# Weight forms made by additions and adding transfers, with no plain units, in a retention and state-space block

## The chip, the cores and the metric

The kernel runs on one core of a Trainium2 chip. The metric is device time in microseconds (us) for one execution; the times shown are medians of several runs. A core has TensorE (matrix products into PSUM), VectorE, ScalarE and GpSimd (elementwise work), SyncE (which issues transfers), and sixteen DMA engines that move the data. In the profile these are PE (with PEld, its weight loads), DVE, ACT, POOL and SP.

## The reference

One layer of a hybrid encoder over 512 positions with 2048 channels, all float32:

```python
h = rmsnorm(x, norm1_w[l])
proj = jnp.einsum('bsd,de->bse', h, w_in[l])
q, k, v, g_ret, z, xbc, dt_raw, gate_r, gate_s = jnp.split(proj, offsets, axis=-1)
y_r = retention(q, k, v, positions) * silu(g_ret)
y_s = ssd(xbc, dt_raw, conv_w[l], conv_b[l], dt_bias[l], a_log[l], d_skip[l])
y_s = rmsnorm(y_s * silu(z), ssd_norm_w[l])
p_r = jnp.einsum('bse,ed->bsd', y_r, w_br_ret[l])
p_s = jnp.einsum('bse,ed->bsd', y_s, w_br_ssd[l])
merged = sigmoid(gate_r) * p_r + sigmoid(gate_s) * p_s
x = x + jnp.einsum('bsd,de->bse', merged, w_out[l])
return rmsnorm(x, norm_f_w)
```

The input projection has 22592 columns: q, k, v and a gate for 8 retention heads of 256; z (4096), xBC (4096 + 2 x 1024) and dt (64) for the state-space branch; two merge gates of 2048. The state-space branch has 64 heads of 64 channels in 8 groups. With a chunk's running sum `acum` of the step sizes times decay rates, its scan computes

```python
decay = jnp.exp(jnp.where(causal, seg, -jnp.inf))        # seg = acum[l] - acum[s]
y = jnp.einsum('blsg,blsgh,bsghp->blghp', cb, decay, xc)  # within a chunk
y = y + jnp.einsum('blgn,bghpn->blghp', cc, state) * jnp.exp(acum)[..., None]
state = state * exp(acum[:, -1]) + einsum('bsgn,bsgh,bsghp->bghpn', bc, tail, xc)
```

where xc is x times its step size and `tail` is the decay from a position to the end of its chunk. The kernel uses chunks of 128 positions here.

## The kernel before

**Products.** Nearly all the work is products of a weight block (2048 deep, 256 columns wide) with activations (2048 deep, 512 positions). One such product is a *unit* (function `unit`). Depth is taken in eight steps k of 256. In each step the weights and the activations are seen as 2 x 2 blocks, two halves of the depth by two halves of the columns or positions, and the product is made by the Strassen-Winograd scheme: seven block products of combined operands in place of eight. The table `SEVEN` lists them as (PSUM bank, half, weight form, activation form). Both operands carry seven forms in a tile's slots 0 to 6: four blocks, and combinations of them. Each form is split into a high part in a reduced format (`hi`, cast on ScalarE at L150) and the rest (`lo`, subtracted on VectorE at L151), and a product is three matmuls, hi x hi, hi x lo, lo x hi (L202 to L204). So a unit issues 8 x 7 x 3 matmuls of 256 columns. After the eight steps, `unit` combines the banks into the four output blocks (L255 to L259).

A *plain* unit makes all eight block products by the table `FOUR`, 8 x 4 x 3 matmuls of 512 columns, and needs no combined weight forms; its outputs are combined at L250 to L252. Which units are plain is set by hand: K and V of head 0 (`PLAIN_K`, `PLAIN_V`), the first of the two x units of each group (`PLAIN_X`), the last merge gate (`PLAIN_M`), and the first and last units of the later projections (`PLAIN2`). The last unit of all is written out by itself (`PASSES`) and is plain in the same sense.

**Weights.** Function `products` loads weights two steps at a time, a pair, into a tile `wf` with `FB` = 3 buffers: two loads of 256 KB on SP (L216), four of 128 KB where B and C share a unit. VectorE then forms slots 4 and 5 (L219), 0 (L221) and 6 (L222) for both steps, and then come the cast and the subtraction for each step, into tiles `whi` (`HB` = 7 buffers) and `wlo` (`LB` = 6). The weight work is issued at a raised priority, ahead of its use. In the last three steps (`LAST`) of a unit the products are ordered by bank, so that the first banks are finished early.

**Activations.** A stage's eight operand groups stay in tiles `hh0` to `hh7` and `hl0` to `hl7` while all of its units run. They have one buffer each, so the next stage's group i is written after the last unit of the stage before has used it. Forms 4 and 6 (`combined`, L155 and L156) are made on GpSimd for seven of the eight groups, forms 5 and 0 (`completed`, L159 and L160) on VectorE.

**Stages.** After the first norm come the 8 retention heads (four units each, with rotary tables, scores, values and a group norm), then 8 state-space groups, each with one unit for B and C, and twice a unit for x, one for z and, but for the first time, one for the merge gates (16 in all); then the projections of the retention output, of the two halves of the state-space output, and the output projection with the last norm.

**The scan.** For each 128 channels of x, a block with two heads, the convolved x is transposed and scaled (`xd`, L622), decayed on GpSimd (`xl`, L625), multiplied with B into the chunk states (L629, L636). For each of the two heads in turn, SP loads the running sums to all partitions (`L`, two buffers, L643), ScalarE makes four differences (L645) and one exponential (L647), VectorE multiplies by CB (L648), and TensorE makes the chunks' outputs (L650), 64 partitions for each head. State outputs (L654), skip, gate and a running sum of squares on GpSimd (L664) follow.

**Order.** Apart from a few sections whose order is written out (`InOrder`), a planner orders each engine's instructions by priority and simulated time when the kernel is built; on the chip each engine then runs its own list in that order.

Of the kernel before, what the change touches and what calls it, by code (L numbers as in the profile page):

```python
# [8 lines left out]
F32 = mybir.dt.float32  # L9
# [57 lines left out]
def constants():  # L67
# [7 lines left out]
    for h in range(NH):  # L75
# [17 lines left out]
SEVEN = (((0, 0, 1, 1), (1, 0, 3, 3), (1, 1, 0, 5)),  # L93
         ((2, 0, 5, 6), (2, 1, 4, 4)),
# [11 lines left out]
PLAIN2 = (0, 7)  # L106
PLAIN_Q, PLAIN_K, PLAIN_V, PLAIN_G = (), (0,), (0,), ()
PLAIN_B, PLAIN_X, PLAIN_Z, PLAIN_M = (), (0,), (), (15,)
# [21 lines left out]
def hybrid_block(tc, A, out):  # L130
# [43 lines left out]
    def rows(src, i):  # L174
        return src[i * 256:(i + 1) * 256, :].rearrange("(r p) t -> p r t", p=P)

# [12 lines left out]
    def products(H, parts, pt, groups, PE=PE, after=None):  # L189
# [17 lines left out]
        for k in range(NP):  # L207
            with tc.high_priority(offset=PRIO):
                if k % 2 == 0:
# [8 lines left out]
                    if not plain:  # L218
                        DVE.tensor_tensor(f2[:, :, 4:6, :], f2[:, :, 1:3, :],  # L219
                                          f2[:, :, 0:1, :].to_broadcast([P, 2, 2, P]), op=ALU.subtract)  # L220
                        DVE.tensor_tensor(f2[:, :, 0, :], f2[:, :, 2, :], f2[:, :, 4, :], op=ALU.add)  # L221
                        DVE.tensor_tensor(f2[:, :, 6, :], f2[:, :, 3, :], f2[:, :, 0, :], op=ALU.subtract)  # L222
# [16 lines left out]
    def unit(H, parts, alt=False, plain=False):  # L239
# [7 lines left out]
        with tc.high_priority():  # L247
            if plain:
                for c in range(2):
                    ACT.copy(o[:, 2 * c:2 * c + 2, :], pt[2 * c][:, 0:1, :].to_broadcast([P, 2, 256]))  # L250
                    DVE.tensor_tensor(o[:, 2 * c, :], pt[2 * c][:, 1, :], o[:, 2 * c, :], op=ALU.add)
                    DVE.tensor_tensor(o[:, 2 * c:2 * c + 2, :], pt[2 * c + 1], o[:, 2 * c:2 * c + 2, :], op=ALU.add)  # L252
            else:
                p1, u = o[:, 0, :], o[:, 0:4:3, :]
                ACT.copy(p1, pt[0][:, 0, :])  # L255
                DVE.tensor_tensor(o[:, 1:3, :], pt[1], p1[:, None, :].to_broadcast([P, 2, 256]), op=ALU.add)  # L256
                DVE.tensor_tensor(u, o[:, 2:3, :].to_broadcast([P, 2, 256]), pt[2], op=ALU.subtract)
                DVE.tensor_tensor(o[:, 2, :], o[:, 0, :], pt[2][:, 1, :], op=ALU.subtract)
                DVE.tensor_tensor(u, pt[3], u, op=ALU.add)  # L259
# [297 lines left out]
    with tc.tile_pool(name="ssd", bufs=1) as sp:  # L557
# [30 lines left out]
        for g in range(NG):  # L588
# [14 lines left out]
            for jj in range(2):  # L603
# [5 lines left out]
                for e in range(2):  # L609
# [15 lines left out]
                    POOL.tensor_tensor(xl, xd[:, :TB - 1], tail[:, :TB - 1, hs, None].to_broadcast([P, TB - 1, 2, 64]),  # L625
# [13 lines left out]
                    pi = att_tile()  # L639
                    for i in range(2):  # L640

                        L = sp.tile([P, TB, P], F32, name="L", bufs=2)
                        SP.dma_start(out=L.rearrange("p c l -> p (c l)"), in_=A_d[h0 + i].partition_broadcast(P))  # L643
                        for c in range(TB):
                            ACT.activation(L[:, c, :], L[:, c, :], AF.Relu, scale=-1.0,  # L645
                                           bias=At[:, c, h0 + i:h0 + i + 1])
                        ACT.activation(L, L, AF.Exp, scale=-1.0)  # L647
                        DVE.tensor_tensor(L, L, CB, op=ALU.mult)  # L648
                        for c in range(TB):
                            PE.matmul(pi[i * 64:(i + 1) * 64, c * P:(c + 1) * P], xd[:, c, i, :], L[:, c, :],  # L650
                                      start=True, stop=True)
# [65 lines left out]
    with tc.tile_pool(name="fin", bufs=1) as fp:  # L717
# [56 lines left out]
        dve.tensor_tensor(t0, o[0][:, 0:2, :], t0, op=ALU.add)  # L774
# [47 lines left out]
```

## Time and profile before

| | |
|---|---|
| median of 3 runs | 2779.19 us (2778.53 to 2781.94) |
| profiled execution | 2779.37 us, of which the span is 2777.6 us |
| mean granted TensorE clock | 0.991 |
| mean rate of all transfers | 131 GB/s |
| read from HBM, written to it | 321.56 MB, 37.49 MB |

The span runs from the first to the last instruction of the one execution that the profiler recorded. In rows of groups, a line names the source line, the engine, the operation, output<-inputs, the shape and the count; then come the busy time in us, the mean of one in ns, and the idle time of the engine just before them with what ended it. Rows of stretches give the busy time of each engine between two times. Rows of waits give the engine and line that waited, whom it waited for, the total in us, the count and the longest.

### The profile page before, as it was taken

Reading aid. Unit: us, or ns where it says so; the run is one execution under the profiler, and the core shown is the slowest. Engines: PE = TensorE matmul, PEld = TensorE weight load, DVE = VectorE, ACT = ScalarE, POOL = GpSimd, SP = SyncE. Lnnn points to the kernel's source line nnn. Section 1 sums busy time; section 2 is a strip of 40 time slices with the busy share of each in tenths; the row PEclk is TensorE's granted clock in tenths of the full one; section 3 lists DMA queues with packets and bytes.
Section 4 is the critical chain, followed back from the end, with each engine's and each line's share of the span. In section 5 each row is a group of like instructions: output and inputs, shape, how many; then the busy total and the mean of one; then the engine's idle time right before and its main releaser. Section 6 shows DMA issues by size and latency. Waiting matters only on the chain.

```text
span 2777.6 us, 52322 instructions
## 1 busy us (share of the span) xinstructions
PE 2715.8 (98%) x20508; PEld 2586.4 (93%) x20508; DVE 2391.4 (86%) x3782; ACT 1336.1 (48%) x1905; POOL 253.1 (9%) x206
## 2 busy tenths in 40 slices
PE   6999999999999999999999999999999999999898
PEld 3899999999989999999999999999989989889797
DVE  8999888888869798898979899797989798898997
ACT  4344333333355555555565555465554343533453
POOL 4000000000000000000000000000021020111321
PEclk9999999999999999999999999999999999999999
DMA  3333333333333434343434434344465554556634
GB/s 125 99 103 104 97 109 103 103 92 103 103 111 114 134 122 133 104 128 117 135 121 135 135 109 126 119 129 120 129 199 168 162 179 137 167 179 194 217 117 137
DMA packets 344375, 362.48 MB, mean 131 GB/s; under 512 B 25664, under 2 KB 298304, under 8 KB 344128
## 3 DMA queue, kind: packets, MB, share of 16 engines
q1 hardware_dynamic: 323888, 325.32, 38.7%
q10 hardware_dynamic: 20240, 33.82, 3.3%
q8 instruction: 161, 2.64, 0.4%
q14 instruction: 86, 0.70, 0.1%
HBM read 321.56 MB, written 37.49 MB: 129 GB/s over the span
## 4 chain that ended last, share of the span: by engine, by line
PE 82%; DVE 8%; DMA 5%; issue 3%; ACT 1%; POOL 1%; SPq 0%; DVEq 0%; POOLq 0%; ACTq 0%
PE pb L204 23%; PE pb L203 23%; PE pb L202 23%; PE att L202 2%; PE att L204 2%; PE att L203 2%; DVE wlo L151 2%; PE att L650 2%; DMA wf<-in_w_in_dram 1%; PE att L536 1%; PE att L521 1%; DMA wf<-in_w_br_ssd_dram 1%; DVE hl L151 1%; PE pb L120 1%; PE att L654 1%
## 5 line engine op out<-in xcount | busy, mean ns | idle before, releaser
L203 PE MATMUL pb<-hl,whi 128*128 128x256 f32 (+1 forms) x5464 | 1601.1, 294 | 11.9 <-DVE hl L120 9.3
L202 PE MATMUL pb<-hh,whi 128*128 128x256 f32 (+1 forms) x5464 | 1596.8, 295 | 9.9 <-ACT hh L150 7.1
L204 PE MATMUL pb<-hh,wlo 128*128 128x256 f32 (+1 forms) x5464 | 1587.9, 294 | 6.0 <-DVE wlo L151 6.0
L150 ACT CAST whi<-wf 128x896 fp32r<-128x896 f32 (+1 forms) x968 | 824.5, 888 | 870.1 <-PE pb L203 396.6
L203 PEld LDWEIGHTS pb<-hl,whi 128*128 128x128 f32 x5464 | 1049.1, 192 | 34.6 <-DVE hl L120 11.0
L202 PEld LDWEIGHTS pb<-hh,whi 128*128 128x128 f32 x5464 | 1046.4, 192 | 33.8 <-ACT hh L150 8.4
L151 DVE TENSOR_TENSOR wlo<-wf,whi 128x896 fp32r<-128x896 f32 (+1 forms) x968 | 1011.8, 1056 | 71.9 <-PE pb L204 30.6
L204 PEld LDWEIGHTS pb<-hh,wlo 128*128 128x128 f32 x5464 | 1041.0, 192 | 28.1 <-DVE wlo L151 6.8
L219 DVE TENSOR_TENSOR wf<-wf 128x512 f32<-128x512 f32 x404 | 281.5, 697 | 159.1 <-DMA wf<-in_w_in_dram 118.8
L202 PE MATMUL att<-hh,whi 128*128 128x256 f32 (+1 forms) x768 | 227.0, 297 | 1.4 <-ACT whi L150 1.4
L203 PE MATMUL att<-hl,whi 128*128 128x256 f32 (+1 forms) x768 | 226.7, 297 | 0.0
L204 PE MATMUL att<-hh,wlo 128*128 128x256 f32 (+1 forms) x768 | 222.7, 297 | 2.0 <-DVE wlo L151 2.0
L221 DVE TENSOR_TENSOR wf<-wf 128x256 f32<-128x256 f32 x404 | 174.3, 432 | 4.0
L222 DVE TENSOR_TENSOR wf<-wf 128x256 f32<-128x256 f32 x404 | 174.0, 431 | 3.1
L202 PEld LDWEIGHTS att<-hh,whi 128*128 128x128 f32 x768 | 147.4, 192 | 6.0 <-ACT whi L150 2.0
L204 PEld LDWEIGHTS att<-hh,wlo 128*128 128x128 f32 x768 | 144.8, 191 | 7.0 <-DVE wlo L151 2.8
L203 PEld LDWEIGHTS att<-hl,whi 128*128 128x128 f32 x768 | 147.5, 192 | 3.9
L645 ACT ACTIVATE L<-L,sst 128x128 f32<-128x128 f32 x256 | 80.3, 394 | 70.3 <-DMA L<-A_d 40.6
L625 POOL TENSOR_TENSOR xl<-xd,sst 128x384 f32<-128x384 f32 x32 | 33.7, 1054 | 864.1 <-DVE xd L622 864.1
L255 ACT COPY o<-pb 128x256 f32<-128x256 f32 x89 | 33.0, 370 | 128.0 <-PE pb L204 117.8
L256 DVE TENSOR_TENSOR o<-pb,o 128x512 f32<-128x512 f32 x89 | 61.0, 685 | 36.2 <-PE pb L204 35.9
L542 POOL TENSOR_TENSOR rs<-rs,mhalf 128x1 f32<-128x1 f32 x32 | 23.9, 751 | 713.3 <-DVE rs L541 704.2
(230 smaller groups left out, 2133.4 us busy)
## 6 DMA issues: line engine op xcount, KB each, us to landing
wf<-in_w_in_dram SPq DMA_DIRECT2D x640, 256.0 KB, 3.1
wf<-in_w_br_ssd_dram SPq DMA_DIRECT2D x128, 256.0 KB, 3.5
wf<-in_w_out_dram SPq DMA_DIRECT2D x72, 256.0 KB, 3.2
wf<-in_w_in_dram SPq DMA_DIRECT2D x128, 128.0 KB, 2.5
L<-A_d SPq DMA_DIRECT2D x64, 256.0 KB, 3.4
wf<-in_w_br_ret_dram SPq DMA_DIRECT2D x64, 256.0 KB, 3.5
ys_d<-B ACTq DMA_DIRECT2D x32, 256.0 KB, 2.5
E<-E_d SPq DMA_DIRECT2D x64, 96.0 KB, 2.7
```

Of the source, the lines that this page charges most:

```text
L150: ACT.copy(dst_hi, src)
L151: DVE.tensor_tensor(dst_lo, src, dst_hi.bitcast(F32), op=ALU.subtract)
L202: PE.matmul(o, wh, xh, start=b not in started, stop=False, skip_group_check=True)
L203: PE.matmul(o, wh, xl, start=False, stop=False, skip_group_check=True)
L204: PE.matmul(o, wl, xh, start=False, stop=(k == NP - 1), skip_group_check=True)
L219: DVE.tensor_tensor(f2[:, :, 4:6, :], f2[:, :, 1:3, :], f2[:, :, 0:1, :].to_broadcast([P, 2, 2, P]), op=ALU.subtract)
L221: DVE.tensor_tensor(f2[:, :, 0, :], f2[:, :, 2, :], f2[:, :, 4, :], op=ALU.add)
L222: DVE.tensor_tensor(f2[:, :, 6, :], f2[:, :, 3, :], f2[:, :, 0, :], op=ALU.subtract)
L256: DVE.tensor_tensor(o[:, 1:3, :], pt[1], p1[:, None, :].to_broadcast([P, 2, 256]), op=ALU.add)
L625: POOL.tensor_tensor(xl, xd[:, :TB - 1], tail[:, :TB - 1, hs, None].to_broadcast([P, TB - 1, 2, 64]), op=ALU.mult)
L645: ACT.activation(L[:, c, :], L[:, c, :], AF.Relu, scale=-1.0, bias=At[:, c, h0 + i:h0 + i + 1])
L650: PE.matmul(pi[i * 64:(i + 1) * 64, c * P:(c + 1) * P], xd[:, c, i, :], L[:, c, :], start=True, stop=True)
```

## The change

- No unit is plain any more: the `PLAIN` lists are empty, so all of `unit`'s products go by `SEVEN`.
- The signs of the scheme are changed, so that each combined weight form is a sum: forms 0 and 5 become sums of two blocks, 4 = new 0 + block 2, 6 = 4 + block 3. The activations' forms and the output additions take the other signs, with the same number of operations. Two entries of `SEVEN` change their weight slots.
- A third transfer on SP brings the first block of each step (512-byte rows) a second time, into slot 5 (`first_tiles`). Then POOL issues one transfer for each of the two steps that adds slots 1 and 2 to slots 0 and 5 on the way (`accum_op`), 128 KB each from SBUF to SBUF. VectorE makes two additions of 256 elements for the pair, where it made one of 512 and two of 256.
- The scan's `L` is one tile for both heads with one buffer, one transfer, one exponential and one product with CB; the matmuls with `xd` go chunk by chunk, the two heads in turn.
- `xl` is made on VectorE instead of GpSimd.

```diff
-SEVEN = (((0, 0, 1, 1), (1, 0, 3, 3), (1, 1, 0, 5)),
-         ((2, 0, 5, 6), (2, 1, 4, 4)),
+SEVEN = (((0, 0, 1, 1), (1, 0, 3, 3), (1, 1, 4, 5)),
+         ((2, 0, 5, 6), (2, 1, 0, 4)),
          ((3, 0, 6, 2), (3, 1, 2, 0)))
...
-PLAIN2 = (0, 7)
-PLAIN_Q, PLAIN_K, PLAIN_V, PLAIN_G = (), (0,), (0,), ()
-PLAIN_B, PLAIN_X, PLAIN_Z, PLAIN_M = (), (0,), (), (15,)
+PLAIN2 = ()
+PLAIN_Q, PLAIN_K, PLAIN_V, PLAIN_G = (), (), (), ()
+PLAIN_B, PLAIN_X, PLAIN_Z, PLAIN_M = (), (), (), ()
...
     def combined(f, eng):
-        eng.tensor_tensor(f[:, 4, :], f[:, 0, :], f[:, 2, :], op=ALU.add)
-        eng.tensor_tensor(f[:, 6, :], f[:, 0, :], f[:, 1, :], op=ALU.subtract)
+        eng.tensor_tensor(f[:, 4, :], f[:, 0, :], f[:, 2, :], op=ALU.subtract)
+        eng.tensor_tensor(f[:, 6, :], f[:, 0, :], f[:, 1, :], op=ALU.add)
 
     def completed(f, eng):
-        eng.tensor_tensor(f[:, 5, :], f[:, 4, :], f[:, 1, :], op=ALU.subtract)
-        eng.tensor_tensor(f[:, 0, :], f[:, 3, :], f[:, 5, :], op=ALU.subtract)
+        eng.tensor_tensor(f[:, 5, :], f[:, 2, :], f[:, 6, :], op=ALU.subtract)
+        eng.tensor_tensor(f[:, 0, :], f[:, 3, :], f[:, 5, :], op=ALU.add)
...
+    def first_tiles(src, i):
+        return src[i * 256:(i + 2) * 256, :P].rearrange("(m r p) t -> p m r t", r=2, p=P)[:, :, 0, :]
...
                     if not plain:
-                        DVE.tensor_tensor(f2[:, :, 4:6, :], f2[:, :, 1:3, :],
-                                          f2[:, :, 0:1, :].to_broadcast([P, 2, 2, P]), op=ALU.subtract)
-                        DVE.tensor_tensor(f2[:, :, 0, :], f2[:, :, 2, :], f2[:, :, 4, :], op=ALU.add)
-                        DVE.tensor_tensor(f2[:, :, 6, :], f2[:, :, 3, :], f2[:, :, 0, :], op=ALU.subtract)
+                        SP.dma_start(out=f2[:, :, 5, :], in_=first_tiles(parts[0], k))
+                        for m in range(2):
+                            POOL.dma_start(out=f2[:, m, 0:6:5, :], in_=f2[:, m, 1:3, :], accum_op=ALU.add)
+                        DVE.tensor_tensor(f2[:, :, 4, :], f2[:, :, 0, :], f2[:, :, 2, :], op=ALU.add)
+                        DVE.tensor_tensor(f2[:, :, 6, :], f2[:, :, 4, :], f2[:, :, 3, :], op=ALU.add)
...
-                    POOL.tensor_tensor(xl, xd[:, :TB - 1], tail[:, :TB - 1, hs, None].to_broadcast([P, TB - 1, 2, 64]),
+                    DVE.tensor_tensor(xl, xd[:, :TB - 1], tail[:, :TB - 1, hs, None].to_broadcast([P, TB - 1, 2, 64]),
                                        op=ALU.mult)
...
+                    L = sp.tile([P, 2, TB, P], F32, name="L")
+                    SP.dma_start(out=L.rearrange("p i c l -> p i (c l)"),
+                                 in_=A_d[hs, :].partition_broadcast(P))
                     for i in range(2):
-                        L = sp.tile([P, TB, P], F32, name="L", bufs=2)
-                        SP.dma_start(out=L.rearrange("p c l -> p (c l)"), in_=A_d[h0 + i].partition_broadcast(P))
                         for c in range(TB):
-                            ACT.activation(L[:, c, :], L[:, c, :], AF.Relu, scale=-1.0,
+                            ACT.activation(L[:, i, c, :], L[:, i, c, :], AF.Relu, scale=-1.0,
                                            bias=At[:, c, h0 + i:h0 + i + 1])
-                        ACT.activation(L, L, AF.Exp, scale=-1.0)
-                        DVE.tensor_tensor(L, L, CB, op=ALU.mult)
-                        for c in range(TB):
-                            PE.matmul(pi[i * 64:(i + 1) * 64, c * P:(c + 1) * P], xd[:, c, i, :], L[:, c, :],
+                    ACT.activation(L, L, AF.Exp, scale=-1.0)
+                    DVE.tensor_tensor(L, L, CB[:, None].to_broadcast([P, 2, TB, P]), op=ALU.mult)
+
+                    for c in range(TB):
+                        for i in range(2):
+                            PE.matmul(pi[i * 64:(i + 1) * 64, c * P:(c + 1) * P], xd[:, c, i, :], L[:, i, c, :],
                                       start=True, stop=True)
```

The output additions in `unit`, and one subtraction in the hand-ordered end, change signs alone.

More of the change, by code (lines that the diff above doesn't have):

```diff
@@ L773, in hybrid_block @@
         act.activation(o[0][:, 2:4, :], t1, AF.Square)
-        dve.tensor_tensor(t0, o[0][:, 0:2, :], t0, op=ALU.add)
+        dve.tensor_tensor(t0, t0, o[0][:, 0:2, :], op=ALU.subtract)
         products(H, last_w, pt, PASSES[1], pe, lambda: sums(0))
```

12 lines of the change are left out of this document (6 added, 6 removed).

## The prediction

> **What bounds the kernel now.** I read the page first, for the share of each engine.
>
> ```profile
> span 2777.6 us, 52322 instructions
> ...
> PE 2715.8 (98%) x20508; PEld 2586.4 (93%) x20508; DVE 2391.4 (86%) x3782; ACT 1336.1 (48%) x1905; POOL 253.1 (9%) x206
> ```
>
> The profiled execution took 2779.4 us, its span and 1.8 us around it; the median of the three timed runs is 2779.19 us, so the sum below is made against 2779.4 and holds for the median too. TensorE is busy 98% of the span. Whether it waits anywhere is shown by stretches; the columns are the length, then PE, PEld, DVE, ACT and POOL busy, the clock, the DMA share and GB/s.
>
> ```profile
> core 0: us, PE busy (x) PEld busy (x) DVE busy (x) ACT busy (x) POOL busy (x), PEclk, DMA share, GB/s
> 61.00:100.00 39.00, 33.33 (x216) 30.02 (x215) 36.05 (x52) 17.04 (x23) 4.43 (x3) 0.91 0.33 96
> ...
> 200.00:830.00 630.00, 626.13 (x4913) 607.98 (x4913) 519.95 (x902) 251.59 (x327) 21.48 (x28) 1.00 0.34 103
> 830.00:2060.00 1230.00, 1229.03 (x9608) 1185.22 (x9607) 1065.76 (x1700) 702.25 (x1111) 82.11 (x66) 1.00 0.42 127
> ...
> 2460.00:2520.00 60.00, 53.81 (x420) 52.80 (x419) 53.43 (x78) 20.46 (x25) 12.88 (x7) 0.94 0.57 180
> 2580.00:2620.00 40.00, 32.86 (x162) 27.46 (x161) 38.38 (x50) 17.11 (x17) 15.45 (x13) 0.87 0.53 162
> 2640.00:2740.00 100.00, 100.00 (x836) 100.00 (x835) 91.50 (x127) 50.80 (x70) 23.43 (x10) 1.00 0.35 111
> ```
>
> Inside the stages (200 to 830 the retention heads, 830 to 2060 the scan, 2640 to 2740 the last projection) TensorE lacks 5 us in 1960. It waits where one stage's operands end and the next one's begin: 5.7, 6.2 and 7.1 us in the three short stretches, with VectorE busy in nine tenths of them (36.05 of 39, 53.43 of 60, 38.38 of 40). So there are two kinds of place. In most of the kernel only TensorE work counts. At the boundaries, VectorE forms eight operand groups and the weight forms at once, and VectorE work counts. Ten of the eighteen plain units stand at these boundaries, eight inside the scan stage.
>
> **Plain units, on TensorE.** A plain unit copies its sums twice at L250, which counts the units; two stretches that hold one kind of matmul alone give the rates.
>
> ```profile
> L250 ACT COPY o<-pb x30: 566/589/592, 77.4 to 2628.6; 128x512 f32<-128x512 f32 x30
> L250 ACT COPY o<-att x6: 573/578/589, 2235.0 to 2588.1; 128x512 f32<-128x512 f32 x6
> ```
> ```profile
> 2400.00:2420.00 20.00, 20.00 (x90) 16.57 (x89) 19.90 (x27) 10.85 (x12) 7.57 (x8) 1.00 0.66 208
> 2140.00:2160.00 20.00, 20.00 (x169) 20.00 (x169) 16.95 (x27) 7.31 (x9) 0.00 (x0) 1.00 0.49 158
> ```
>
> 36 copies are 18 units: K and V of head 0, eight x units, the last merge gate, and seven first and last units of the projections. A window also counts the two matmuls still running as it opens, so 20 us hold 88 matmuls of 512 columns (0.227 us each) and 167 of 256 (0.120 us). A plain unit has 8 x 4 x 3 = 96 of the wide ones, 21.8 us; a unit of seven products 8 x 7 x 3 = 168 narrow ones, 20.2 us. 18 units at 1.6 us make **-29 us**. Were every boundary unit paced by VectorE instead, only the eight x units would gain, 13 us: these are the ends.
>
> **What VectorE gets.**
>
> ```profile
> L151 DVE TENSOR_TENSOR wlo<-wf,whi 128x896 fp32r<-128x896 f32 x808 | 894.5, 1117 | 46.7 <-ACT whi L150 21.6 <-PE pb L204 19.1 <-ACT o L584 3.5
> L150 ACT CAST whi<-wf 128x896 fp32r<-128x896 f32 x808 | 728.4, 941 | 731.5 <-DVE wf L222 314.9 <-PE pb L203 291.4 <-issue 39.2
> L219 DVE TENSOR_TENSOR wf<-wf 128x512 f32<-128x512 f32 x404 | 281.5, 697 | 159.1 <-DMA wf<-in_w_in_dram 118.8 <-DMA wf<-in_w_br_ssd_dram 25.3 <-DMA wf<-in_w_br_ret_dram 8.0
> ...
> L221 DVE TENSOR_TENSOR wf<-wf 128x256 f32<-128x256 f32 x404 | 174.3, 432 | 4.0
> ...
> L151 DVE TENSOR_TENSOR wlo<-wf,whi 128x512 fp32r<-128x512 f32 x160 | 118.1, 747 | 25.2 <-PE pb L204 11.5 <-issue 4.6 <-ACT whi L150 2.6
> L150 ACT CAST whi<-wf 128x512 fp32r<-128x512 f32 x160 | 97.0, 621 | 138.6 <-PE pb L203 105.2 <-PE att L203 7.7 <-PE att L204 7.3
> ```
>
> A pair of weight blocks costs VectorE 0.70 + 2 x 0.43 = 1.56 us of forms now and 2 x 0.43 = 0.86 us after, four pairs a unit: a unit that already has seven products loses 2.8 us. A former plain unit gains 4 x 0.86 + 8 x (1.117 - 0.747) = 6.4 us; its output additions stay four of much the same shapes, counted as nothing. Over the kernel: -101 x 2.8 + 18 x 6.4 = -168; decayed x moves here, 384 elements at no more than the 0.75 us of 512 in L151, 32 x 0.75 = +24 at most; 32 products with CB of 1024 elements replace 64 of 512, counted as nothing (896 elements at 1.12 us cost less than two times 512 at 0.75). VectorE falls from 2391 to about 2250 us. ScalarE gains 144 casts x 0.32 = 46 us on 1336, hidden, as it is half idle.
>
> At the boundaries the same rows count the other way: two plain units become heavier (+12.8 us of VectorE), their two neighbours lighter (-5.6): +7 us at each of four boundaries, and about +10 at the start (K and V against Q): at most 38 us, if VectorE sets the pace throughout. At least it is nothing, if the spare VectorE time before the boundary takes it. The quoted stretches are neither free nor full (11 us idle of 139), and forms of operands can't be made early, because their buffers are those of the stage before; I take half, **+19 us**.
>
> **The scan's matmuls.** The change issues the two heads' chunks alternately, and they fill different halves of TensorE's columns (the output's partitions 0 to 63 and 64 to 127).
>
> ```profile
> 867.47 1.58 PE L650 MATMUL att<-L,xd 128*64 128x128 f32 x16
> ```
> ```profile
> 867.40:867.94 0.54, 0.47 (x4) 0.48 (x5) 1.00 0.00 0
> 867.94:868.28 0.34, 0.34 (x8) 0.34 (x8) 1.00 0.00 0
> ```
>
> This is one block now. Its first four records take 0.47 us, 0.11 us each or more. In the next 0.34 us eight run, of which two began before: six starts, 57 ns apart. That is where the planner already mixes the heads. With all sixteen at 57 ns a block takes 16 x 0.057 + 0.28 = 1.2 us, not 1.58: 0.4 us x 32 blocks = **-13 us**; nothing at one end, if the order comes out as now. The Trainium skill's TensorEngine Tiling (Array Packing), section Theoretical Speedup, gives up to 2x for a dimension of at most 64; by half of all 1.58 us the term would be -25 and the sum 2744, but this trace shows half of the block overlapped already.
>
> Both heads' L now share one buffer and one transfer, so the second block of a pair loads only after the first block's matmuls, and weight loads queue behind it on SP.
>
> ```profile
> SPq L216 <- DVE wlo L151: 1244.9, 335, 11.6
> ...
> SPq L643 <- PE att L650: 115.5, 37, 5.4
> ```
>
> SP already waits so in 37 of 64 loads, 3 us each, and TensorE runs through it in the scan. Half as many loads with a longer wait: taken at nothing, 115 us of SP at most, covered by three units of product work per pair of blocks.
>
> **The adding transfers.** A third load on SP, two transfers issued by POOL that wait for all three loads, and VectorE's forms behind them: the loop of a weight buffer gets longer. There are three buffers, and the rows above say that loads wait for a buffer most of the time.
>
> ```profile
> 876.54 0.89 SPq L216 DMA_DIRECT2D wf<-in_w_in_dram  x2
> ```
> ```profile
> wf<-in_w_in_dram SPq DMA_DIRECT2D x640, 256.0 KB, 3.1
> ...
> wf<-in_w_in_dram SPq DMA_DIRECT2D x128, 128.0 KB, 2.5
> ...
> f<-m_d SPq DMA_DIRECT2D x16, 256.0 KB, 4.4
> ```
> ```profile
> L542 POOL TENSOR_TENSOR rs<-rs,mhalf 128x1 f32<-128x1 f32 x32 | 23.9, 751 | 713.3 <-DVE rs L541 704.2 <-DVE mv L540 8.4 <-DVE mv L544 0.8
> ```
>
> Loads: the third starts 0.9 us after the first and lands 3.1 later, 4.0 us. Then the forms 0.86, the first cast 0.94, two low parts 2.2: 8.0 us plus the adding pair. The trace has no transfer of POOL. At the low end it is like 128 KB on SP, one issue of 0.45 and 2.5: 3 us. At the high end each issue takes two of POOL's smallest instructions (0.75 us for one column) and the landing is the slowest here, 4.4: 7 us. I take 4.5 (two issues of 0.75 and a landing of 3, nearest to the weight loads). The loop is then 12.5 us. TensorE uses up three pairs in 20.2 x 3 / 4 = 15.1 us, and the hi and lo buffers hold six to seven blocks more; so the transfers hide, at **0**. Behind a waiting transfer in POOL's queue stand the operand forms, the squares' sum, the gates and the small powers; behind VectorE's wait for it the low parts and the output sums.
>
> **Sum.** 2779.4 - 29 - 13 + 19 = **2756 us**.
>
> **Rivals.**
>
> The weight loop becomes the bound (slower). It decides from an adding pair plus queueing of 7.1 us. At 7 us and 1.5 us of waiting behind busy engines the loop is 16.5, a unit takes 22.0 us: +1.8 on each of the 31 units of the last stages, +0.5 on the 56 units of the scan stage (1230 us over 56, less their own gains, is 21.5), 84 us in all: 2840. For it: VectorE already waits for loads (159 us at L219), and POOL issues in order. Against: 4 us of slack at my value. Chance 0.20.
>
> The transfer engines fill up (slower).
>
> ```profile
> q1 hardware_dynamic: 323888, 325.32, 38.7%
> q10 hardware_dynamic: 20240, 33.82, 3.3%
> ```
> ```profile
> 2049.00:2740.00 691.00, 669.80 (x4806) 633.40 (x4805) 607.50 (x856) 294.85 (x359) 114.65 (x83) 0.99 0.54 171
> ```
>
> q1's packets took 53 ns for 1004 bytes, q10's 73 for 1671 (share x 16 x 2777.6 / count); a line through both gives 39 ns for 512, an estimate. A unit adds 4 x 256 rows of first tiles and 8 x 256 added rows: 2.5 and 5.0 us on each engine, or 10 if an added row is read twice. Of 20.2 us that is 12% and 25 to 50%, on 54% in the last stages: 0.91 to 1.16. From 53 ns per added row it decides; at 1.16 the last 691 us grow by 110: 2866. The Trainium skill's DMA: Bandwidth & Descriptors, section Issuing engines are not separate DMA queues, says the same: transfers from POOL share the 16 engines with SP's. No run here shows an added row's time. Chance 0.10.
>
> The boundaries take the whole 38 us: 2779 - 42 + 38 = 2775, about no change. Chance 0.13.
>
> VectorE's relief also ends the waits of the boundary stretches (19 us) and nothing is added there: 2779 - 42 - 19 = 2718. Chance 0.07.
>
> **How the numbers follow.** The forecast has 0.50, its own range 2737 (no boundary cost) to 2780 (no gain in the scan's matmuls, boundaries at 30). 8 in 10 reach from 2725 (most of the last rival out, 0.05) to 2850 (filled engines and a worse loop out, 0.15). About 0.2%, 5.6 us, can be told from no change. Faster: 0.47 of the forecast, 0.07, and 0.03 of the boundary case, 0.57. Same: 0.03 and 0.06, 0.09. Slower: 0.20, 0.10 and 0.04, 0.34.
>
> **What would show it.** Right: 256-column matmuls 120 ns apart through all units, no L250, a block of L650 in about 1.2 us, VectorE near 2250 us, and TensorE's waits only at boundaries, some 40 us. Wrong: VectorE's first form waiting hundreds of us on POOL's transfers with TensorE waiting behind it inside the last stages (the loop); landings of weight loads far over 3.1 us at a DMA share near 1 (full engines); or L650 still at 1.6 us.

## The result, and the profile after

The changed kernel takes 4362.55 us (median of 4 runs, 4356.76 to 4369.25) where the kernel before takes 2778.86 in the same measurement: a ratio of 1.570, interval 1.568 to 1.572. The forecast of 2756 us was wrong in sign, and its range ended at 2850. The profiled execution took 4357.91 us, with a span of 4356.1.

From the page of the changed kernel, the engines, the DMA engines' busy tenths by slices (40 slices of 109 us), the transfer queues and four groups:

```profile
span 4356.1 us, 58671 instructions
...
PE 3171.6 (73%) x21804; PEld 3025.5 (69%) x21804; DVE 2243.8 (52%) x3522; ACT 1358.1 (31%) x1857; POOL 1333.7 (31%) x1126
...
DMA  4555555555555556666555555655566565666654
...
q1 hardware_dynamic: 448752, 387.73, 30.1%
q0 software_dynamic: 258944, 124.84, 24.9%
...
L210 PE MATMUL pb<-hh,whi 128*128 128x256 f32 x5824 | 1816.8, 315 | 528.3 <-ACT o L265 198.3
L230 POOL DMA_DIRECT2D wf<-wf x952 | 1157.1, 1215 | 2909.4 <-issue 1931.1
...
L231 DVE TENSOR_TENSOR wf<-wf 128x256 f32<-128x256 f32 x476 | 203.5, 428 | 1787.9 <-issue 1348.1
L155 DVE TENSOR_TENSOR wlo<-wf,whi 128x896 fp32r<-128x896 f32 (+1 forms) x968 | 1042.4, 1094 | 145.2 <-ACT whi L154 105.0
```

TensorE was busy 98% and is busy 73%. It idles 1184.5 us where it idled 61.8, and its busy time rose by 456 us, though its products are less work: the matmuls went at a lower mean clock, 0.844 against 0.991 (3171.6 x 0.844 and 2715.8 x 0.991 are the same within 1%). No other engine is full: VectorE 52%, ScalarE 31%, POOL 31%, the sixteen DMA engines four to six tenths. With time to spare on every engine, what sets the pace has to be looked for in the waits. TensorE has 181 gaps of over 3 us here, 881 us in all, where it had 6. The Trainium skill's TensorE: Matmul & The Clock Gate, section Why this matters for your kernels, says that gaps of over about 3 us between bursts of matmuls lower the clock; this trace agrees, with those gaps and a clock of 0.82 to 0.86 in the three stretches below.

The stretches of the changed kernel (length; PE, PEld, DVE, ACT, POOL busy; clock, DMA share, GB/s) show that the time is not lost at boundaries, as the prediction's small losses would be, but everywhere alike:

```profile
200.00:1000.00 800.00, 591.15 (x4012) 559.39 (x4012) 384.38 (x677) 191.68 (x249) 229.75 (x200) 0.85 0.52 108
1000.00:3000.00 2000.00, 1485.33 (x10539) 1430.18 (x10540) 1035.02 (x1645) 719.71 (x1070) 592.22 (x487) 0.86 0.57 123
3200.00:4300.00 1100.00, 778.58 (x5180) 748.20 (x5179) 561.71 (x794) 291.14 (x332) 372.20 (x323) 0.82 0.63 146
```

Its waits (who waited, for whom, us in total, times, longest) name the loop:

```profile
POOL wf L230 <- issue: 1931.1, 713, 7.2
ACT whi L154 <- DVE wf L232: 1743.2, 270, 19.3
DVE wf L231 <- issue: 1348.1, 339, 8.7
DVE wf L231 <- DMA wf<-wf: 439.8, 111, 9.0
```

ScalarE's casts wait for VectorE's form 6 (L232), VectorE's form 4 (L231) for POOL's adding transfers or for "issue", and POOL before its transfers (L230) for "issue": nothing that the profile shows. For form 4 the trace settles it: all 407 waits of over 1 us ended 0.08 to 0.45 us after the landing of that pair's second transfer. POOL's timeline (start, length, operation, idle before it) shows both transfers of a pair and the first of the next, and the list of transfers what one takes to land:

```profile
1019.99 1.21 POOL L230 DMA_DIRECT2D wf<-wf  x1 [3.96 <-issue]
1023.50 1.22 POOL L230 DMA_DIRECT2D wf<-wf  x1 [2.30 <-issue]
1027.02 1.21 POOL L230 DMA_DIRECT2D wf<-wf  x1 [2.30 <-issue]
```
```profile
wf<-wf POOLq DMA_DIRECT2D x952, 128.0 KB, 3.2
```

The second transfer of a pair starts 3.5 us after the first (median 3.51, none under 3.43; 295 of the 476 pairs lie between 3.4 and 3.6, the others later). POOL is busy 1.2 us and then stands for 2.3, until the first has landed (3.2, the median of all): the second starts 0.26 to 0.32 us after that landing in every pair, and not one of the 952 transfers starts with another still under way. So it gets out one transfer at a time. That is a rate: 2 x 3.5 = 7.0 us for a pair of weight blocks, of which TensorE uses up one in 20.2 / 4 = 5.05 us. 476 pairs at 7.0 are 3340 us by themselves. The span is 1000 us longer still, so the rate is a floor and not the whole of it; what else goes into the loop of a weight buffer is measured further below.

### The profile page after: what moved, and what is told of

The parts are those of the page before. It is cut to its first block, busy times and chain, and to the rows that moved or that the text cites. A ratio compares the mean times of both kernels' runs of the same rounds, so it can differ in the third digit from the quotient of the medians.

```text
span 4356.1 us, 58671 instructions
## 1 busy us (share of the span) xinstructions
PE 3171.6 (73%) x21804; PEld 3025.5 (69%) x21804; DVE 2243.8 (52%) x3522; ACT 1358.1 (31%) x1857; POOL 1333.7 (31%) x1126
## 3 DMA queue, kind: packets, MB, share of 16 engines
q0 software_dynamic: 258944, 124.84, 24.9%
## 5 line engine op out<-in xcount | busy, mean ns | idle before, releaser
L210 PE MATMUL pb<-hh,whi 128*128 128x256 f32 x5824 | 1816.8, 315 | 528.3 <-ACT o L265 198.3
L230 POOL DMA_DIRECT2D wf<-wf x952 | 1157.1, 1215 | 2909.4 <-issue 1931.1
L212 PE MATMUL pb<-hh,wlo 128*128 128x256 f32 x5824 | 1781.4, 311 | 168.9 <-DVE wlo L155 168.8
L211 PE MATMUL pb<-hl,whi 128*128 128x256 f32 x5824 | 1795.1, 309 | 61.9 <-DVE hl L124 38.8
L210 PEld LDWEIGHTS pb<-hh,whi 128*128 128x128 f32 x5824 | 1265.9, 219 | 575.3 <-ACT o L265 209.3
L212 PEld LDWEIGHTS pb<-hh,wlo 128*128 128x128 f32 x5824 | 1259.7, 218 | 185.3 <-DVE wlo L155 184.4
L211 PEld LDWEIGHTS pb<-hl,whi 128*128 128x128 f32 x5824 | 1274.6, 219 | 68.2 <-DVE hl L124 40.6
L231 DVE TENSOR_TENSOR wf<-wf 128x256 f32<-128x256 f32 x476 | 203.5, 428 | 1787.9 <-issue 1348.1
L155 DVE TENSOR_TENSOR wlo<-wf,whi 128x896 fp32r<-128x896 f32 (+1 forms) x968 | 1042.4, 1094 | 145.2 <-ACT whi L154 105.0
L212 PE MATMUL att<-hh,wlo 128*128 128x256 f32 x840 | 249.2, 315 | 82.4 <-DVE wlo L155 82.3
L210 PE MATMUL att<-hh,whi 128*128 128x256 f32 x840 | 262.5, 315 | 54.8 <-ACT whi L154 54.8
L211 PE MATMUL att<-hl,whi 128*128 128x256 f32 x840 | 258.6, 311 | 0.0
L210 PEld LDWEIGHTS att<-hh,whi 128*128 128x128 f32 x840 | 186.1, 222 | 59.4 <-ACT whi L154 59.2
L232 DVE TENSOR_TENSOR wf<-wf 128x256 f32<-128x256 f32 x476 | 201.8, 426 | 5.1
```

Source lines behind the costliest of these rows:

```text
L155: DVE.tensor_tensor(dst_lo, src, dst_hi.bitcast(F32), op=ALU.subtract)
L210: PE.matmul(o, wh, xh, start=b not in started, stop=False, skip_group_check=True)
L211: PE.matmul(o, wh, xl, start=False, stop=False, skip_group_check=True)
L212: PE.matmul(o, wl, xh, start=False, stop=(k == NP - 1), skip_group_check=True)
L230: POOL.dma_start(out=f2[:, m, 0:6:5, :], in_=f2[:, m, 1:3, :], accum_op=ALU.add)
L231: DVE.tensor_tensor(f2[:, :, 4, :], f2[:, :, 0, :], f2[:, :, 2, :], op=ALU.add)
```

## The experiments

Three theories stood for POOL's standing still. A: the space for its transfers' descriptors, which the kernel sets where it is built (`dynamic_dma_scratch_size=1024`, L825), holds one adding transfer of 256 rows and not two. B: adding transfers go one at a time whatever the space. C: the DMA engines are the bound, since an added row takes long.

**Space for two: e1_ring1088.**

```diff
-    nc = bacc.Bacc("TRN2", target_bir_lowering=False, num_devices=1, dynamic_dma_scratch_size=1024)
+    nc = bacc.Bacc("TRN2", target_bir_lowering=False, num_devices=1, dynamic_dma_scratch_size=1088)
```

> The descriptor space for POOL's transfers grows from 1024 to 1088 bytes of a partition, from 64 to 68 entries of 16 bytes; nothing else changes. Theory A (space): an adding transfer of 256 rows puts 16 rows on each engine and needs two reads a row and one entry for the semaphore, 33, so 64 entries hold one transfer and 68 hold two; the second transfer of a pair then starts 1.2 us after the first instead of 3.5, and the time falls from 4360 to 2900 to 3500 us. Theory B (POOL finishes each transfer before it issues the next, whatever the space): 3.5 us between starts and about 4360 us. Theory C (the 16 engines are the bound, 70 ns for each added row): about 4360 us, the landings only get longer.

Measured: 3403.66 us (a single run), 959 us less, for 64 bytes in one constant. From its waits:

```profile
POOL wf L230 <- DMA wf<-in_w_in_dram: 471.0, 120, 17.1
...
POOL wf L230 <- issue: 193.9, 143, 4.1
```

POOL's 1931 us without a reason are 194 now, and the second transfer starts 0.75 us after the first (median). By the trace at most two are ever under way, where it was one. A holds; B falls, and C as the cause of this part. One adding transfer takes over 512 bytes (two don't fit in 1024) and at most 544 (two fit in 1088). From the Trainium skill a count can be worked out that lies between: an add needs two reads for each piece (Collectives: The Full Stack, section The bandwidth ceiling: the fold count and why AG ≠ RS ≠ AR), and a descriptor has 16 bytes (DMA: Bandwidth & Descriptors, section Terms); 256 rows on sixteen engines, read twice, and one more at the end make 33 x 16 = 528, an estimate. The trace has 272 packets for an adding transfer (258944 / 952), 17 for each engine; a second read doesn't show in it.

**Copies instead of additions: e3_copy.**

```diff
-                            POOL.dma_start(out=f2[:, m, 0:6:5, :], in_=f2[:, m, 1:3, :], accum_op=ALU.add)
+                            POOL.dma_start(out=f2[:, m, 0:6:5, :], in_=f2[:, m, 1:3, :])
```

> The transfers on POOL copy blocks 1 and 2 into slots 0 and 5 instead of adding them; the sums of those two forms are left out. A plain copy needs one read a row, 17 entries. Theory A: three fit into 64 entries, so starts come 1.2 us or less apart and the time is 2780 to 3000 us with the space as it was. Theory B: 3.5 us between starts and over 4000 us. Theory C: shorter rows, perhaps 40 ns instead of 70, so the time falls in part, to 3300 to 3900 us, with starts close together.

Measured: 3046.56 us (a single run). The page's group and the queue of POOL's transfers:

```profile
q0 software_dynamic: 45696, 124.84, 12.5%
...
L230 POOL DMA_DIRECT2D wf<-wf x952 | 689.7, 726 | 1935.0 <-DMA wf<-in_w_in_dram 432.1 <-DVE wlo L155 365.2 <-DVE wf L232 242.2
```

In the same 1024 bytes two copies go out 0.72 us apart, and "issue" is gone from the group's first reasons (19.6 us of it are left), as A has it. The time is a little over the 2780 to 3000 us that A gave. A copy takes POOL 0.73 us, an addition 1.2, and moving the same bytes took the engines 0.125 x 16 x 3044.8 = 6.1 ms of engine time as copies, against 0.249 x 16 x 4356.1 = 17.4 ms as additions. More than the adding differs here: a copy went out in 48 packets (45696 / 952), 32 of them with 4096 bytes, and not in rows of 512. So it needed far fewer than the expected 17 entries for each engine; this run agrees with A, but it is e1 that shows it.

**More space: e2_ring1600.** The same constant at 1600, which holds three.

> 1600 bytes, 100 entries. Theory A: three transfers of 33 fit, so no start waits for a landing, 1.2 us between the two of a pair, and the time falls to 2780 to 3000 us; what is left is set by the engines' time, as added rows at 70 ns make 1080 us on each engine beside about 1400 us of the other transfers, nine tenths of 2800 us. Theory B and C: about 4360 us.

Measured: 3333.82 us, ratio 1.202 (1.200 to 1.204). Another 70 us. That is above the 2780 to 3000 us that A gave: the space was the cause of POOL's standing still, but not of all the loss. At most three transfers are under way by the trace, and "issue" before POOL's transfers is down to 31.0 us, so more space has little left to give. POOL's timeline:

```profile
1018.86 2.46 POOL L230 DMA_DIRECT2D wf<-wf  x2 [2.08 <-DMA wf<-in_w_in_dram]
1022.91 2.44 POOL L230 DMA_DIRECT2D wf<-wf  x2 [1.60 <-DVE xd L632]
```

Both transfers of a pair go out together, and what POOL waits for has a name. The kernel is still 557 us above the one before.

**No transfers at all: e4_dve_forms.** VectorE makes the two sums.

```diff
-                        SP.dma_start(out=f2[:, :, 5, :], in_=first_tiles(parts[0], k))
-                        for m in range(2):
-                            POOL.dma_start(out=f2[:, m, 0:6:5, :], in_=f2[:, m, 1:3, :], accum_op=ALU.add)
+                        DVE.tensor_tensor(f2[:, :, 5, :], f2[:, :, 0, :], f2[:, :, 2, :], op=ALU.add)
+                        DVE.tensor_tensor(f2[:, :, 0, :], f2[:, :, 0, :], f2[:, :, 1, :], op=ALU.add)
```

> The third load and the transfers on POOL go; VectorE makes the two forms by two additions of 256 elements for a pair (0.86 us), everything else as changed: no plain units, scan by blocks, decayed x on VectorE. Theories A to C: the transfers are the whole loss, and the time is 2740 to 2800 us, 120 ns between matmuls. Theory D (the loss is in the missing plain units or in the scan's single L buffer): over 3000 us.

Measured: 2858.35 us, ratio 1.029 (1.028 to 1.031). So of the change's 1584 us the transfers make 1504 (the adding ones and the third load together), and 80 are lost by its other parts; 2740 to 2800 had been expected, with nothing lost there.

**Half the transfers: e6_one_form**, at 1024 bytes: one adding transfer a pair, of the same 256 rows (form 5 of both steps), and form 0 on VectorE.

```diff
-                        for m in range(2):
-                            POOL.dma_start(out=f2[:, m, 0:6:5, :], in_=f2[:, m, 1:3, :], accum_op=ALU.add)
+                        POOL.dma_start(out=f2[:, :, 5, :], in_=f2[:, :, 2, :], accum_op=ALU.add)
+                        DVE.tensor_tensor(f2[:, :, 0, :], f2[:, :, 0, :], f2[:, :, 1, :], op=ALU.add)
```

> As changed, with 1024 bytes, but one adding transfer for a pair that makes form 5 alone (256 rows); VectorE adds form 0 (0.43 us a pair). Theory A: one transfer fits and there is none behind it in the same pair, so the loop is 4 us of loads and waiting, 4.5 to 5 of the transfer, 2 of forms, 6.5 of splitting, 17 to 18.5 us, and the time 2800 to 3000 us. A theory by which any adding transfer costs, whatever the count: over 3300 us.

Measured: 2980.53 us, ratio 1.072 (1.069 to 1.075). One transfer of 3.5 us fits into the 5.05 us of a pair even one at a time, and the great loss is gone without more space; 122 us above e4 stay, for half of the additions and for the third load, which e4 leaves out as well.

**What holds the rest: the loop of a raw buffer.** From the traces, the mean times of a pair, from the issue of its first load to the end of its last low part, in us:

| kernel | first load to first transfer | to the second | to form 4 | forms 4 and 6 | to the first cast | to the end of the last low part | loop |
|---|---|---|---|---|---|---|---|
| predicted | 4.0 | 0.75 | 3.75 | 0.86 | 0 | 3.14 | 12.5 |
| after | 8.59 | 3.93 | 4.16 | 1.86 | 0.56 | 7.80 | 26.9 |
| e3_copy | 5.71 | 0.76 | 4.01 | 1.79 | 0.66 | 5.72 | 18.7 |
| e2_ring1600 | 5.83 | 0.85 | 5.27 | 1.79 | 0.69 | 6.03 | 20.5 |
| e5, four buffers | 6.14 | 0.90 | 5.49 | 2.00 | 2.65 | 9.61 | 26.8 |
| e9, four and order | 6.16 | 0.88 | 10.86 | 1.60 | 0.40 | 4.02 | 23.9 |
| e12, three and order | 5.96 | 0.80 | 6.40 | 1.54 | 0.28 | 3.76 | 18.7 |

Three buffers go round once in the loop's time, so 484 pairs take 484 / 3 loops: 26.9 gives 4340 us, 18.7 gives 3020 and 20.5 gives 3307, against spans of 4356, 3045 and 3331. With four buffers the product comes out as well (e5: 3243 of 3270; e9: 2892 of 2926, where TensorE is 94% busy). So it says that a raw buffer is filled again as soon as it is free, and not yet what holds it. That is told by the waits: in the changed kernel the casts wait 1743 us for VectorE's forms and 236 for TensorE's products of earlier blocks. There the loop sets the time, and TensorE follows.

**A fourth raw buffer: e5_ring1600_4wf**, with e2's space, paid for by one `hi` and one `lo` buffer. Theory L: the loop's length over the number of buffers; theory S: the transfers get longer as more are in flight.

```diff
-FB, HB, LB = 3, 7, 6
+FB, HB, LB = 4, 6, 5
```

> As e2 (1600 bytes), with four buffers for the raw weights instead of three, paid for with one hi and one lo buffer less (6 and 5). Theory L (the loop of a raw weight buffer is the bound that is left in e2: 20.5 us from the first load's issue to the last low part, over three buffers 6.8 us a pair, 484 pairs 3300 us): with four buffers the same loop gives 2500 us, less than TensorE needs, so the time falls to 2850 to 2980 us. Theory S (the shared transfer engines are the bound: share 0.70 to 0.81 in e2): the loop grows to 27 us and the time stays within 5% of 3334.

Measured: 3276.13 us, ratio 1.178 (1.177 to 1.180): only 58 us less than e2. L as it was put fell, since the loop grew with the buffers; S fell too, since the transfers' own legs did not (0.90 and 5.49 us against 0.85 and 5.27). What grew are the legs behind the forms. One part is the price of the buffer: with six `hi` buffers for seven, the casts wait 508 us for TensorE's products where they waited 199 in e2, most of it in one row:

```profile
ACT whi L154 <- PE pb L211: 361.7, 149, 9.3
```

With the same six buffers and another order (e9, below) it is 165, so most of this wait hangs on the order as well. What the order does can be seen in the trace of the changed kernel, on ScalarE and on VectorE:

```profile
1021.87 1.78 ACT L154 CAST whi<-wf 128x896 fp32r<-128x896 f32 x2 [9.01 <-DMA wf<-in_w_in_dram]
```
```profile
1026.78 0.42 DVE L231 TENSOR_TENSOR wf<-wf 128x256 f32<-128x256 f32 x1 [3.87 <-issue]
1027.12 1.08 DVE L155 TENSOR_TENSOR wlo<-wf,whi 128x896 fp32r<-128x896 f32 x1
```

The casts of one pair end at 1023.65. Their low parts (L155) could follow, but in VectorE's list form 4 (L231) of a later pair stands ahead of them, and VectorE stands 3.87 us for that pair's transfers. The first low part starts at 1027.12, 3.5 us after both casts have ended, and the raw buffer is held as long. Counted over the traces, low parts of earlier pairs were still behind form 4 in 307 of 476 places with three buffers. With four it was so in 466 of 476, two or more of them in 444, and VectorE was idle for 780 us in all just before those 444. The planner's order is made when the kernel is built, from simulated times; that the wait comes out longer than these is argued here, not read from them.

**The order put right: e9_forms_last and e12_forms_last_3wf.** Form 4 of a pair follows the last low part of the pair before it on VectorE; e9 with four raw buffers (against e5), e12 with three (against e2).

```diff
-                        DVE.tensor_tensor(f2[:, :, 4, :], f2[:, :, 0, :], f2[:, :, 2, :], op=ALU.add)
+                        form4 = DVE.tensor_tensor(f2[:, :, 4, :], f2[:, :, 0, :], f2[:, :, 2, :], op=ALU.add).ins
+                        if low:
+                            tc.add_manual_dep(
+                                form4, low[-1].name,
...
-                split(hi[:, :n, :], lo[:, :n, :], f[:, :n, :])
+                low.append(split(hi[:, :n, :], lo[:, :n, :], f[:, :n, :]))
```

> As e5 (1600 bytes, four raw buffers), with VectorE's order fixed so that a pair's forms come after both low parts of the pair before. In e5 VectorE idles 830 us at the forms, waiting for POOL's transfers with two or three ready low parts behind it in 441 of 476 pairs. Theory O (VectorE waits in order for transfers that land later than its order assumes): the idle time before the forms falls by more than half and the time to 2850 to 3050 us. Theory S (shared transfer engines set the pace): 3200 to 3350 us, with the wait moved elsewhere.

> As e2 (1600 bytes, three raw buffers, seven hi and six lo), with VectorE's order fixed as in e9. In e2 the loop of three buffers takes 20.5 us, and VectorE waits at the forms also where no low part is left behind it (302 us in 169 pairs), which no order mends. If both matter, the order over three buffers gives 3050 to 3250 us, between e2 (3334) and e9 (2930). If the order alone was the cause: 2900 to 2960 us. If the order helps only with a fourth buffer: 3300 us or more.

Measured: e9 2930.48 us, ratio 1.055 (1.054 to 1.057); e12 3068.45 us, 1.107 (1.105 to 1.109). The order alone is worth 265 us with three buffers (e2 to e12) and 346 with four (e5 to e9); the fourth buffer 58 without the order and 138 with it. The waits of VectorE's form 4 in e5 and in e9 (where it is L233):

```profile
DVE wf L231 <- issue: 573.7, 229, 7.4
...
DVE wf L231 <- DMA wf<-wf: 215.5, 76, 6.6
```
```profile
DVE wf L233 <- issue: 17.0, 14, 2.9
DVE wf L233 <- DMA wf<-wf: 15.2, 5, 8.1
```

789 us of waiting became 32. In e9 form 4 comes 10.9 us after the transfer instead of 5.5, later and no longer waited for, and the low parts end 4.0 us after the first cast instead of 9.6. The scan stage of e9:

```profile
830.00:2060.00 1230.00, 1173.28 (x9741) 1150.21 (x9740) 990.95 (x1511) 687.83 (x1040) 547.54 (x442) 0.99 0.86 185
```

TensorE is near full again, and the DMA share is 0.86 where it was 0.42 in the kernel before.

**The plain units: e8_before_no_plain and e10_forms_last_plain.** The kernel before with the lists emptied and its own forms; and e9 with the lists as before.

```diff
-PLAIN2 = (0, 7)
-PLAIN_Q, PLAIN_K, PLAIN_V, PLAIN_G = (), (0,), (0,), ()
-PLAIN_B, PLAIN_X, PLAIN_Z, PLAIN_M = (), (0,), (), (15,)
+PLAIN2 = ()
+PLAIN_Q, PLAIN_K, PLAIN_V, PLAIN_G = (), (), (), ()
+PLAIN_B, PLAIN_X, PLAIN_Z, PLAIN_M = (), (), (), ()
```

> The kernel before with empty lists of plain units and its old forms on VectorE. My terms: -29 on TensorE, and at the boundaries each former plain unit costs VectorE 9.2 us more (four pairs at 1.56 and eight low parts at 0.37), 18 us a boundary and 90 in all if VectorE paces them: 2750 at one end, 2840 at the other; 2800 to 2840 if VectorE paces them, as the stretches before suggest (busy nine tenths).

> As e9, with the plain units of the kernel before put back, so 404 pairs have transfers instead of 476 and VectorE has its relief at the boundaries. If the boundaries are paced as before the transfers came (e8: empty lists cost 53 us there): 50 to 80 us less than e9. If what is left in e9 is spread evenly over pairs with transfers: 15% of e9's excess over 2780 less.

Measured: e8 2831.83 us, ratio 1.018 (1.017 to 1.020), 53 us slower; e10 2834.11 us, 1.020 (1.018 to 1.021), 96 us faster than e9. In both surroundings the plain units pay; the 96 us are more than either expectation for e10 gave (50 to 80, or some 22). Page and stretches of e8, and below them one stretch of the kernel before:

```profile
PE 2713.7 (96%) x21804; PEld 2651.3 (94%) x21804; DVE 2538.1 (90%) x3998; ACT 1360.4 (48%) x1883; POOL 298.0 (11%) x206
```
```profile
100.00:200.00 100.00, 83.58 (x645) 80.62 (x645) 86.02 (x155) 35.63 (x45) 3.06 (x4) 0.91 0.26 80
...
830.00:2060.00 1230.00, 1228.67 (x10268) 1214.08 (x10267) 1136.86 (x1812) 724.45 (x1117) 97.54 (x63) 1.00 0.42 126
2049.00:2740.00 691.00, 631.03 (x5006) 622.63 (x5005) 631.84 (x902) 285.90 (x324) 128.24 (x80) 0.95 0.52 165
```
```profile
100.00:200.00 100.00, 100.00 (x715) 93.89 (x714) 93.96 (x175) 39.79 (x50) 2.39 (x4) 1.00 0.33 99
```

Inside the scan stage nothing is lost. At the start TensorE lacks 16 us where it lacked none, and in the last stages 60 where it lacked 21, at a clock of 0.95 where it was 0.99. TensorE's idle time rose by 56 us, and its busy time fell by 2 and not by 29: the lower clock took that gain back (4% of 631 us is 25, an estimate).

**The scan part, and the x units: e7_before_scan and e11_before_scan_x.** e7 is the kernel before with the one `L`, one exponential, one product with CB and the two heads' matmuls in turn. e11 also empties the list of x units alone:

```diff
-PLAIN_B, PLAIN_X, PLAIN_Z, PLAIN_M = (), (0,), (), (15,)
+PLAIN_B, PLAIN_X, PLAIN_Z, PLAIN_M = (), (), (), (15,)
```

> The kernel before with the scan part of the change alone: one L tile, one load, the two heads' matmuls in turn. My term: -13 us, a block of L650 in 1.2 us instead of 1.58, 2765 us. Rival: the single buffer's wait stops weight loads behind it on SP and shows in TensorE: 2780 us or more.

> The kernel before with the scan part of the change, and with the eight plain x units made units of seven products, the plain units at the boundaries kept. My terms: -12 (e7) and -13 for eight units at 1.6 us, 2754 us. Rival: VectorE, nine tenths busy in the scan stage and 9.2 us heavier in each such unit, paces it: 2767 to 2790.

Measured: e7 2767.44 us, ratio 0.9955 (0.9943 to 0.9968); e11 2752.69 us, 0.9904 (0.9890 to 0.9918), faster than both kernels. The matmuls of the scan's output, by groups, in the kernel before and in e7 (busy us, mean ns of one):

```profile
L650 PE MATMUL att<-L,xd 128*64 128x128 f32 x512 | 54.7, 279 | 0.0
```
```profile
L653 PE MATMUL att<-L,xd 128*64 128x128 f32 x512 | 35.0, 279 | 1.2 <-issue 1.1
```

One matmul is as long as before, 279 ns, but 32 blocks keep TensorE busy 35.0 us instead of 54.7: 1.09 us a block. The eight x units then bring 15 us more.

**The whole difference in steps**, each between two kernels that were run but for the third, which is what e4 lost beyond the first two, if these add up there:

| step | from, to | us |
|---|---|---|
| scan part | before, e7 | -12 |
| no plain units, old forms | before, e8 | +53 |
| the rest of e4 (four additions for three, decayed x on VectorE) | e4 less both | +38 |
| transfers in place of VectorE's sums, order right, space enough | e4, e12 | +210 |
| VectorE's order | e12, e2 | +265 |
| descriptor space | e2, after | +1029 |

## Why the prediction was wrong

**The step that failed** is the one on the adding transfers: "so the transfers hide, at **0**". It failed in three ways, and they lie on top of each other.

First, it put the pair of transfers as a length in a loop, "two issues of 0.75 and a landing of 3", with both in flight together. They were not: 3.5 us apart at the least, for want of descriptor space. At its shortest the pair, 3.5 + 3.2 = 6.7 us, even lies within the bounds of 3 to 7; in the mean it took 3.93 + 4.16 = 8.1, over the 7.1 from which the first rival decides. Held apart, the transfers cost the loop 6.4 us (26.9 against 20.5 in e2): 3.1 between the two, 2.8 before the first, which stands in the same queue, and 1.6 at the casts and low parts, less 1.1 before form 4. That is +1029 us (e2, after). What the prediction also lacked is the other reading of the same numbers: how many can pass in a given time. Two at 3.5 us are 7.0 for each 5.05 us of TensorE work, 3340 us at the least, which by this sum no number of buffers mends. With three buffers the loop is longer than that, 26.9 / 3 = 9.0 us a pair, and it set the time.

Second, the loop was summed with every engine ready when its operand came. The prediction named what stands "behind VectorE's wait for it", the low parts and the output sums, and priced it at nothing. The low parts are in the loop themselves: an engine that stands at one pair's transfers holds up the buffers of the pairs before it, and the loop's 3.1 us of cast and low parts came to 8.4. That is +265 us (e2, e12).

Third, the margin. With both set right the loop still has 18.7 us and not 12.5, and the limit was 15.1: 6.0 to the first transfer instead of 4.0, 6.4 from the second to form 4 instead of 3.75. That is +210 us (e4, e12). Why these two legs are longer was not taken apart.

The first rival, the weight loop as the bound, was the right mechanism, with 1.5 us of waiting behind busy engines where more than ten came, and so with 2840 us. The second rival, full transfer engines, had the price of an added row about right from its own estimate (39 to 78 ns): q0's packets took 0.249 x 16 x 4356.1 us / 258944 = 67 ns. But the kernel was held up long before the engines were full: their share was 0.57 in the middle of it. In e9, where the loop is mended, it is 0.95 from 2200 to 2850 us, within the 0.91 to 1.16 of that rival, and TensorE lacks 62 of these 650 us; whether for that reason was not tested.

**Plain units**, "-29 us", with boundaries at "+19 us" and at most 38. All 18 units together cost 53 us in e8 instead of saving 10. The end "were every boundary unit paced by VectorE instead, only the eight x units would gain, 13 us" was the right one (e11: 15). The 38 us at most counted VectorE's additional work, in which a pair has 0.86 us of forms. In e8 it has 1.56, so the bound was not tried there. With the transfers in their best order (e9, e10) the 18 units came out dearer still, 96 us, in which the transfers of 72 more pairs are counted too. And the sum left out that a TensorE that waits is also slower, which took back the 29.

**VectorE** was to fall to about 2250 us and has 2243.8. It didn't help: what waited for VectorE waited for forms that VectorE could not make before the transfers had landed. ScalarE gained 22 us, where 46 were reckoned, hidden in either case.

**The scan's matmuls**, -13 us: right, in size and mechanism (-12; a block in 1.09 us where 1.2 was forecast). Half of all 1.58 us a block, which the prediction put beside it from the Trainium skill, would have been -25; the trace's own spacing was the better guide. **L with a single buffer**, taken at nothing: 32 blocks shorter by 0.49 us are 16 us, of which 12 arrived, so it cost about 4 us (in e7 TensorE's busy time fell by 16.5 us and its idle time rose by 4.2).

**What stays open.** The transfers in the best form tried still cost about 70 us against VectorE making the sums (e9 against e4: 72; e10 against e7, which has the same plain units: 67). Whether that is the share of the DMA engines (0.86 in the scan stage), the third load, the fourth buffer taken from the `hi` and `lo` tiles, or the length of the loop was not separated. The 38 us of e4's rest were not taken apart by a run either. More work on VectorE (1.72 us of forms a pair against 1.56) is only argued, and it would not be at the boundaries alone: from 830 to 2060 us, in the scan stage, TensorE lacks 23.7 us in e4 and 1.3 in e8, from 2049 to 2740 us 69.8 and 60.0.

## What to carry to other kernels

Before work is handed to transfers that POOL issues, ask two things of them: how long one takes in the loop of its buffer, and how many can be under way at once, which here hung on a constant that had no part in the change. A POOL that stands before its next transfer with nothing named as the reason, until the one before has landed, is the sign of it. A loop's length is not enough, either: a buffer's loop and the rate of its transfers are two bounds, and both have to be set against TensorE's 5.05 us a pair. And where an in-order engine gets a longer wait, look at what stands ready behind it: the order, which an added wait makes wrong, cost 265 us here, and a fourth buffer without it bought 58. A change of several parts is best undone part by part: two of these parts, the scan's and the x units, are worth 26 us together.

## What the runs showed of the hardware

- Adding transfers of 256 rows of 512 bytes take over 512 and at most 544 bytes of the space set for POOL's descriptors; a transfer that doesn't fit is held until the one before it has landed (it starts 0.26 to 0.32 us after that, 3.5 us from start to start; 0.73 where it fits). At most one was under way with 1024 bytes, two with 1088, three with 1600.
- POOL is busy for 1.2 us with an adding transfer and 0.73 us with a copy of the same size; landing takes 3.2 us with one in flight, and 4.1 where two go out together (e2).
- An adding transfer kept the DMA engines busy 2.8 times as long as a copy of the same bytes (17.4 ms against 6.1). The added rows went as packets of 512 bytes, 70 ns each; the copies, from the same access patterns, as packets of 4096 bytes, 196 ns each. A 512-byte packet of the loads' queue (q1) took 29 ns in the same trace as the added rows.
- With TensorE idle for 27% of the span its granted clock was 0.844, and matmuls of 256 columns had a mean of 315 ns (L210) where the kernel before has 285 (L202, clock 0.991); so a TensorE that waits also works more slowly. The single records of the clock are either 1.0 or 0.5: 1358 us of the changed kernel at 0.5, 54 us of the kernel before.
